# Two products for three in stick-breaking attention: the second parts of the split queries and values on the idle half of the array

## The chip, the cores and the metric

One core of one Trainium2 chip runs the whole program. The metric is the device time of one execution in microseconds (us); lower is better. Engines are named as in the profile: PE (TensorE matmul), PEld (its weight load), DVE (VectorE), ACT (ScalarE), POOL (GpSimd), SP (SyncE, which issues the loads).

## The reference

Two transformer blocks over 512 tokens of 1024 features. The first mixer runs stick-breaking attention (8 heads of 64) and HGRN2 (4 heads of 128) side by side and adds both, gated; the change touches the attention alone:

```
z = einsum('bhqd,bhkd->bhqk', qi, k) * scale        # blocks of 128 queries
log_beta = log_sigmoid(z)
log_rem = where(mask, log_beta - z, 0.0)            # mask: key before query
between = cumsum(log_rem, reverse) - log_rem
w = where(mask, exp(log_beta + between), 0.0)
o = einsum('bhqk,bhkd->bhqd', w, v)
```

After the first mixer come a squared-relu MLP, then the second block (MLA with a context, MLP, gMLP, MLP). None of that is edited.

## The kernel before

Activations lie feature-major, 128 features by 512 tokens. A float32 operand of a wide product is split into hi (12 significant bits) and lo = x - hi, and `mm3` (L180 to L185) adds hi.hi + hi.lo + lo.hi: three matmuls for one product. Weights come in granules of 128x1024; `wload` splits each with an ACT cast (`wh<-wr`) and a DVE subtraction (`wl<-wr,wh`).

The first mixer is `mixer_one` (L601). `feat` (L642) makes one feature tile: 24 matmuls into one of two PSUM banks (`ps`), then one DVE multiplication by the norm (`fiqg<-ps,rstd`, `qkv<-ps,rstd`, `gate<-ps,rstd`), which also frees the bank. `sb_pair` (L707) is one pair of attention heads (four pairs) in steps: `start` (L711) splits q, k and v; `weights` (L727) makes z of one head and one block of 128 queries with 128, 256, 384 or 512 keys (at least 256 columns are computed), its sigmoids, a DVE scan and a DVE product `b<-b,u`; `turn` (L746) transposes the weights on PE into `wT`; `product` (L756) splits `wT` tile by tile (512, 384, 256, 128 columns) and adds up `o`. A head has 64 features, half of the array's 128 rows. Before, q of a head lies in its half of two tiles, hi and lo, with zeros in the other half (`qz`), and v likewise (`vz`, half of the 128 columns zero), so that both heads add into the two halves of one bank `o`; one ACT copy (L769) takes it out.

`hgrn` (L814) is one head of HGRN2 in steps: features, gates (transposes `vt`), a DVE scan `bc` (L854), `edges` (transposes `kt`, products `sp`), scores `sc`. `branch` (L674) then splits the four `osb` tiles and multiplies them (`pg`).

The order of the steps is the string `ORDER` (L37), written by hand; from it a scheduler with a model of its own orders the queue of each engine. Each engine takes its queue strictly in order. Pools: `P()` is the ring of two `ps` banks, `O()` one of two banks for `z`, `vt`, `sp` and `sc`, and `o` has one bank.

Of the kernel before, what the change touches and what calls it, by code (L numbers as in the profile page):

```python
"""Two transformer blocks on one core.

The first block: stick-breaking attention and HGRN2 side by side, gated, then a squared-relu MLP and a
final norm.  The second: MLA with a context, then a gMLP mixer, each followed by a squared-relu MLP, all
modulated.  What the second block does to the context after its keys and values are taken never reaches
the output, so it is left out.

Activations lie feature-major, [128 features, 512 tokens].  A float32 operand x of a wide product is
split into hi = round(x) to 12 significant bits (the float32r format) and lo = x - hi, which is exact;
hi.hi + hi.lo + lo.hi is accumulated in float32.  Products with few columns run in plain float32.  # L10
"""
# [18 lines left out]
T = 512  # L30
TC = 256
EPS = 1e-6
#: The order in which the steps of the mixer take their turns: pairs of heads of the stick-breaking attention (S), heads
#: of HGRN2 (H), the gates of either branch (A, B) and their projections (G, M).
# [31 lines left out]
def cut(rs, c):  # L66
    """A part of the tokens of split operands."""
    return [(h[:, c], l[:, c]) for h, l in rs]
# [14 lines left out]
class Kernel:  # L83
# [5 lines left out]
    def S(self, n=T, dt=F32, name="t"):  # L89
        """A tile that may outlive the phase."""  # L90
        return self.sp.tile([128, n], dt, tag="s", name=name)

    def H(self, name="t"):
        """Half of the tokens, not for long."""
        return self.hp.tile([128, TC], F32, tag="h", name=name)

    def F(self, n=T, dt=F32, name="f", tag="f"):
        """A tile of the phase, 2 KB in each partition for the common tag."""
        return self.fp.tile([128, n], dt, tag=tag, name=name, bufs=self.tags.get(tag))
# [11 lines left out]
    def phase(self, name, banks, **tags):  # L111
        """Memory of a phase; banks, tags: how many tiles of each kind, in PSUM and in SBUF."""
# [29 lines left out]
    def split(self, x, gain=None, n=T, tag=None, eng=None):  # L142
        """x, times a gain by partition, in two parts."""
        if tag is None:
            hi, lo = self.S(n, F32R, "hi"), self.S(n, F32R, "lo")
        else:
            hi, lo = self.F(n, F32R, "hi", tag), self.F(n, F32R, "lo", tag)
        self.split_into(hi, lo, x, gain, eng)
        return hi, lo
# [7 lines left out]
    def wload(self, src):  # L157
        """One granule of weights, [128, up to 1024], split in two."""
# [7 lines left out]
    def wkeep(self, src):  # L166
        """The stationary operands of a granule that outlives the ring, in tiles of the phase."""
# [6 lines left out]
    def wsplit(self, w, k, c=128):  # L174
        """The stationary operands of k row tiles in a granule."""
# [3 lines left out]
    def mm3(self, out, ls, rs, start=True, stop=True):  # L179
        """out += sum over pairs of ls[i]^T rs[i], every operand a (hi, lo)."""  # L180
# [6 lines left out]
    # Where one layer's output becomes the next one's normed input, the products run half of the tokens at a time, in  # L187
    # a given order on the tensor engine, with the few products of the norm between them.
# [10 lines left out]
    def later(self, n, f):  # L199
        """Calls f after n more products of mm3."""  # L200
# [19 lines left out]
    class Sum:  # L220
        """A running sum of squares over the tiles of a feature-major array; with gains, [128, tiles, (1, gain^2)],
        also one of the squares times the gain's."""
# [18 lines left out]
        def half(self, x, z, m):  # L241
            """The same for half of the tokens of one of the last tiles."""
# [8 lines left out]
        def collect(self, out, z):  # L251
            """The sums over the features, in PSUM; two columns for each 128 tokens."""
# [10 lines left out]
    def sums(self, acc, n=T, bank=None):  # L263
        """The sums over the features of [128, n], tokens on partitions: two equal columns for each 128 tokens."""
# [5 lines left out]
    def rsqrt(self, out, x, d):  # L270
        """out = 1 / sqrt(x / d + eps) of a few columns."""
# [5 lines left out]
    def newton(self, out, a):  # L277
        """out = 1 / sqrt(a) of a few columns: a guess from the bits, then three steps of Newton's."""
# [8 lines left out]
    def spread(self, c, n=T, bank=None, i=0):  # L287
        """Columns, number i of two for each 128 tokens, along the free axis of every partition; in PSUM."""
# [8 lines left out]
    def rstd(self, acc, d, n=T, bank=None):  # L297
        """1 / sqrt(sum over features / d + eps), the same in every partition; in PSUM."""
# [4 lines left out]
    def mod_gain(self, norm, m, which):  # L303
        """norm * (1 + scale) as columns."""
# [7 lines left out]
    def first(self, ps, ws, xs):  # L312
        """Products of a few granules, half of the tokens at a time."""
# [6 lines left out]
    def down(self, srcs, rs, bank, residual, sums, done, whole=4, begun={}):  # L320
        """Output tiles, added to the residual; the last ones half of the tokens at a time.  sums: running sums of
        squares of the residual, with gains; done(z, columns) turns them into half of the next norm."""
# [38 lines left out]
    def renorm(self, norm, m, which):  # L361
        """What `down` calls when a half of the residual is complete: its modulated norm, in self.xs."""
# [11 lines left out]
    def modulate(self, out, xs, r, gains, shifts, c):  # L374
        """Part c of the tokens: (x * gain) * r + shift, split."""
# [12 lines left out]
    def context(self):  # L388
        """Latent keys and values of the context."""
# [49 lines left out]
    def ada(self, layer, lo, hi):  # L439
        """Columns lo..hi of the modulation of a layer, in granules of 128."""  # L440
# [19 lines left out]
    def mlp(self, w1, w2, xs, residual, scale=None, extra=None, down=None, halves=True):  # L460
        """residual(m, psum, tokens) is called with the four partial sums of every output tile."""
# [86 lines left out]
    def mlp_one(self):  # L548
# [30 lines left out]
        # y = h * gf * r goes on, r = 1 / sqrt(mean(h^2) + eps); for 1 / sqrt(mean(y^2) + eps) times r, which is  # L579
        # 1 / sqrt(mean((h * gf)^2) + eps (mean(h^2) + eps)), no second pass is needed  # L580
# [20 lines left out]
    def mixer_one(self):  # L601
        nc, tc, a = self.nc, self.tc, self.a
        xs, ssq, ws = [], self.Sum(self), {}
        # the first operands in pieces, two row tiles of three granules and of x at a time
# [13 lines left out]
        # the tensor engine's clock rises while the first operands are on their way  # L618
# [10 lines left out]
        # the first products, every tile of x as it comes  # L629
# [12 lines left out]
        def feat(m, name="u", tag="f"):  # L642
            """A feature tile of the input projection."""
# [9 lines left out]
        # stick-breaking attention  # L653
        qz = [self.F(T, F32R, "qz", "qv") for _ in range(4)]
        vz = [self.F(T, F32R, "vz", "qv") for _ in range(4)]
        for i in range(4):
            nc.gpsimd.memset((qz[i][64:128] if i < 2 else qz[i][0:64]).bitcast(F32), 0.0)
            o = 64 if i < 2 else 0
            nc.gpsimd.memset(vz[i].rearrange("p (t c) -> p t c", c=128)[:, :, o:o + 64].bitcast(F32), 0.0)
# [3 lines left out]
        for p in range(4):  # L663
            self.sb_pair(p, do, feat, qz, vz, osb)
            self.hgrn(p, do, feat, ohg)

        # the gates of either branch, what they let through of the first, and the sum
# [39 lines left out]
    def sb_pair(self, p, do, feat, qz, vz, out):  # L707
        """Two heads of the stick-breaking attention, in steps."""
        nc, s = self.nc, {}

        def start():  # L711
            q, k, v = s[0], s[1], s[2]
            s["ks"] = self.split(k, tag="sb")
            for h in range(2):
                c = slice(64 * h, 64 * h + 64)
                hi, lo = qz[2 * h], qz[2 * h + 1]
                self.act(hi[c], q[c], AF.Copy, scale=0.125)
                self.stt(lo[c], q[c], 0.125, hi[c].bitcast(F32), ALU.mult, ALU.subtract)
# [3 lines left out]
            for h in range(2):  # L722
                c = slice(64 * h, 64 * h + 64)
                hi, lo, src = (x.rearrange("p (t c) -> p t c", c=128)[:, :, c] for x in (*vz[2 * h:2 * h + 2], vt))
                self.split_into(hi, lo, src)

        def weights(h, i):  # L727
            ks = s["ks"]
# [4 lines left out]
            self.mm3(ps[:, :nn], [(qz[2 * h][:, c], qz[2 * h + 1][:, c])], [(ks[0][:, :nn], ks[1][:, :nn])])  # L733
# [12 lines left out]
        def turn(h, i):  # L746
            if i == 0:
                # transposed weights of the key tiles, 512, 384, 256 and 128 columns in three banks
# [7 lines left out]
        def product(h):  # L756
            if h == 0:
                s["o"] = self.Q("o", "o")
            o = s["o"]
            for j in range(4):  # L760
                n = T - 128 * j
                w = self.split(s["wT"][j][:, :n], n=n)
                vs = [(x.rearrange("p (t c) -> p t c", c=128)[:, j]) for x in vz[2 * h:2 * h + 2]]
                nc.tensor.matmul(o[:, 128 * j:], vs[0], w[0], start=h == 0 and j == 0, stop=False)
                nc.tensor.matmul(o[:, 128 * j:], vs[0], w[1], start=False, stop=False)
                nc.tensor.matmul(o[:, 128 * j:], vs[1], w[0], start=False, stop=h == 1 and j == 3)
            if h == 1:
                r = self.S(name="osb")
                nc.scalar.copy(r, o)  # L769
                self.tap("osb%d" % p, [o])  # L770
                out[p] = r
# [13 lines left out]
    def hgrn_begin(self):  # L785
# [12 lines left out]
        # the lower bound of the forget gate  # L798
# [15 lines left out]
    def hgrn(self, h, do, feat, out):  # L814
        """One head of HGRN2, in steps."""
# [26 lines left out]
        def decay():  # L842
            """Running sums of log f, in two parts for the range that the table takes."""
# [13 lines left out]
        def edges():  # L857
            q, k, b = s[2], s["k"], s["b"]
            # decays from and to the ends of a chunk
# [612 lines left out]
```

## Time and profile before

| what | value |
|---|---|
| runs | 2115.7, 2118.17, 2119.0 us; median 2118.17 |
| span of the profiled execution | 2115.3 us (first to last instruction; the 2.9 us to the median lie around it and between executions) |
| PE, DVE, ACT, POOL busy | 2074.1, 1342.9, 876.1, 216.3 us |
| chain that ended last | PE 87%, DVE 7%, ACT 3%, issue 2%, DMA 1% |
| mean granted clock of PE | 0.996 |

The profile records no device time of its own for the profiled execution, only the span. "Busy" is the time in which an engine has an instruction in flight. Matmuls are pipelined, so the cost of one in a dense run is the distance between the starts of two, not its duration. The windows give the busy time of each engine in a stretch; an engine's timeline gives its instructions one after the other, with the idle time before one and what ended it.

### The profile page before, as it was taken

The numbers are of one execution on the slowest core, as the hardware profiler recorded it, in microseconds if no ns is written. First come the engines' busy times: TensorE is split into PE (matmuls) and PEld (weight loads), VectorE is DVE, ScalarE is ACT, GpSimd is POOL, SyncE is SP. The second block draws the span as 40 slices with busy tenths as digits, with TensorE's granted clock in tenths as the row PEclk, the third lists the DMA queues.
The fourth block names the chain that finished last, engine by engine and source line by source line (L and its number), as shares of the span: only waits on it lengthen the run. The fifth ranks groups of instructions, "written<-read, shape, count | busy, mean of one in ns | idle before, by whom it ended". The sixth has DMA issues, their size and how long they took to land.

```text
span 2115.3 us, 27506 instructions
## 1 busy us (share of the span) xinstructions
PE 2074.1 (98%) x10550; PEld 1759.0 (83%) x10550; DVE 1342.9 (63%) x2482; ACT 876.1 (41%) x1430; POOL 216.3 (10%) x234
## 2 busy tenths in 40 slices
PE   9999999999999999899989999999999999999999
PEld 7888888878888888788878888888888889888887
DVE  6868775689675557888767766646456446434433
ACT  5546663354242324667645423223333324323221
POOL 0313220000000001345311000000000001000000
PEclk9999999999999999999999999999999999999999
DMA  5212122456556432101033655533222231222222
GB/s 173 70 60 66 49 84 63 155 177 208 168 189 199 159 110 87 38 18 36 31 130 112 202 194 196 192 130 119 81 99 80 90 120 61 100 99 91 100 100 80
DMA packets 73908, 238.69 MB, mean 113 GB/s; under 512 B 8240, under 2 KB 12592, under 8 KB 73776
## 3 DMA queue, kind: packets, MB, share of 16 engines
q1 hardware_dynamic: 73776, 236.93, 34.0%
q8 instruction: 83, 1.36, 0.3%
q14 instruction: 49, 0.40, 0.1%
HBM read 232.70 MB, written 4.19 MB: 112 GB/s over the span
## 4 chain that ended last, share of the span: by engine, by line
PE 87%; DVE 7%; ACT 3%; issue 2%; DMA 1%; POOL 0%; SPq 0%; ACTq 0%; DVEq 0%; POOLq 0%
PE pq L184 35%; PE ps L184 28%; PE po L184 13%; PE pg L184 2%; PE sc L215 1%; ACT pr L131 1%; PE pl L215 1%; DVE wl L125 1%; PE pq L215 1%; PE o L184 1%; DVE lo L125 1%; PE z L184 1%; DVE lo L128 1%; PE po L215 1%; PE pl L184 1%
## 5 line engine op out<-in xcount | busy, mean ns | idle before, releaser
L136 ACT CAST wh<-wr 128x1024 fp32r<-128x1024 f32 (+3 forms) x338 | 333.6, 990 | 850.0 <-PE pq L184 423.2
L125 DVE TENSOR_TENSOR wl<-wr,wh 128x1024 fp32r<-128x1024 f32 (+3 forms) x338 | 390.3, 1156 | 113.4 <-ACT wh L136 106.3
L184 PE MATMUL pq<-hi,wl 128*128 128x512 f32 (+1 forms) x880 | 336.2, 382 | 0.0
L184 PE MATMUL pq<-hi,wh 128*128 128x512 f32 (+1 forms) x880 | 336.1, 382 | 0.0
L184 PE MATMUL pq<-lo,wh 128*128 128x512 f32 (+1 forms) x880 | 336.0, 382 | 0.0
L184 PE MATMUL ps<-hl,wh 128*128 128x512 f32 (+1 forms) x752 | 227.6, 384 | 0.0
L184 PE MATMUL ps<-hi,wh 128*128 128x512 f32 x536 | 211.9, 396 | 4.1 <-ACT hi L131 2.1
L184 PE MATMUL ps<-hi,wl 128*128 128x512 f32 x536 | 211.5, 395 | 0.5 <-DVE wl L125 0.5
L184 PE MATMUL ps<-lo,wh 128*128 128x512 f32 x536 | 210.7, 393 | 0.0
L184 PEld LDWEIGHTS pq<-hi,wl 128*128 128x128 f32 x880 | 165.4, 188 | 32.3
L184 PEld LDWEIGHTS pq<-hi,wh 128*128 128x128 f32 x880 | 165.4, 188 | 32.2
L184 PEld LDWEIGHTS pq<-lo,wh 128*128 128x128 f32 x880 | 165.4, 188 | 32.2
L450 DVE SCALAR_TENSOR_TENSOR adaj<-ada,silu 128x1024 bf16<-128x1024 f32 x112 | 137.0, 1223 | 83.4 <-DMA ada<-in_ada 83.0
L128 DVE SCALAR_TENSOR_TENSOR x<-pq,m,x 128x512 f32<-128x512 f32 (+1 forms) x88 | 60.7, 690 | 198.2 <-PE pq L184 197.9
L184 PE MATMUL po<-hl,wh 128*128 128x512 f32 x528 | 163.8, 392 | 0.0
L184 PEld LDWEIGHTS ps<-hl,wh 128*128 128x128 f32 x752 | 139.0, 188 | 27.0
L125 POOL TENSOR_TENSOR hl<-mod,hl 128x256 fp32r<-128x256 f32 x36 | 30.1, 845 | 1164.7 <-ACT hl L382 945.9
L184 PE MATMUL ps<-hl,wl 128*128 128x512 f32 (+1 forms) x376 | 144.1, 383 | 0.0
L184 PEld LDWEIGHTS ps<-hi,wh 128*128 128x128 f32 x536 | 100.7, 188 | 26.2 <-ACT hi L131 2.5
L184 PEld LDWEIGHTS ps<-hi,wl 128*128 128x128 f32 x536 | 100.9, 188 | 22.3 <-DVE wl L125 1.0
L184 PEld LDWEIGHTS ps<-lo,wh 128*128 128x128 f32 x536 | 101.0, 188 | 20.2 <-DVE lo L125 0.4
L184 PEld LDWEIGHTS po<-hl,wh 128*128 128x128 f32 x528 | 99.5, 189 | 20.5
(375 smaller groups left out, 3832.1 us busy)
## 6 DMA issues: line engine op xcount, KB each, us to landing
wr<-in_f SPq DMA_DIRECT2D x128, 512.0 KB, 3.2
ada<-in_ada SPq DMA_DIRECT2D x96, 512.0 KB, 4.1
wr<-in_ff SPq DMA_DIRECT2D x64, 512.0 KB, 4.1
wr<-in_w_in SPq DMA_DIRECT2D x41, 512.0 KB, 3.5
wr<-in_gw_v SPq DMA_DIRECT2D x16, 512.0 KB, 3.2
wr<-in_gw_u SPq DMA_DIRECT2D x16, 512.0 KB, 3.2
wr<-in_gw_o SPq DMA_DIRECT2D x16, 512.0 KB, 3.2
wr<-in_w_out SPq DMA_DIRECT2D x8, 512.0 KB, 3.4
```

What stands on the lines that cost most here:

```text
L125: (eng or self.nc.vector).tensor_tensor(out=out, in0=a, in1=b, op=op)
L128: (eng or self.nc.vector).scalar_tensor_tensor(out=out, in0=a, scalar=s, in1=b, op0=op0, op1=op1)
L131: self.nc.scalar.activation(out=out, in_=x, func=func, scale=scale, bias=bias, **k)
L136: nc.scalar.copy(hi, x)
L184: self.nc.tensor.matmul(out, l, r, start=start and i == j == 0, stop=stop and i == n - 1 and j == 2)
L215: self.nc.tensor.matmul(out, l, r, start=start, stop=stop)
L450: nc.vector.scalar_tensor_tensor(out=d, in0=w, scalar=1.0, in1=s, op0=ALU.mult, op1=ALU.mult, accum_out=m[:, n:n + 1])
```

## The change

The idle half of a tile now carries the other part of the same operand. `qhl[h]` has q hi on the head's 64 partitions and q lo on the other 64. `kh[h]` has k hi on both halves, so one matmul gives q hi.k hi + q lo.k hi; a second one with `klz[h]` (k lo, zeros in the other half) adds q hi.k lo. `vhl[h]` has v hi in 64 columns and v lo in the other 64; one matmul with w hi and one with w lo give both parts in the two halves of PSUM, which are added while they are copied out (w lo.v lo comes along). Each head so takes a bank of its own, one after the other, since `o` still has one.

Counts: z takes 2 matmuls for 3 in 32 places, o likewise: 64 fewer on PE. Of these 32, the z ones have 256, 384 and 512 columns (16, 8, 8), the o ones 128, 256, 384 and 512 (8 each). DVE has 12 instructions more (per pair: `klz` twice where one `lo<-qkv,hi` stood, and two additions `osb<-o,ol`), ACT 18 more (per pair three more copies for `kh`, and two copies `ol<-o` for one `osb<-o`; two more table loads), POOL 6 memsets fewer. SP's loads are the same.

```
-        qz = [self.F(T, F32R, "qz", "qv") for _ in range(4)]
-        vz = [self.F(T, F32R, "vz", "qv") for _ in range(4)]
...
+        qhl, klz, vhl = ([self.F(T, F32R, n, "qv") for _ in range(2)] for n in ("qhl", "klz", "vhl"))
+        for h in range(2):
+            nc.gpsimd.memset(klz[h][64 - 64 * h:128 - 64 * h].bitcast(F32), 0.0)
...
         def start():
-            s["ks"] = self.split(k, tag="sb")
+            s["kh"] = [self.F(T, F32R, "kh", "sb") for _ in range(2)]
             for h in range(2):
-                c = slice(64 * h, 64 * h + 64)
-                hi, lo = qz[2 * h], qz[2 * h + 1]
-                self.act(hi[c], q[c], AF.Copy, scale=0.125)
-                self.stt(lo[c], q[c], 0.125, hi[c].bitcast(F32), ALU.mult, ALU.subtract)
+                c, e = slice(64 * h, 64 * h + 64), slice(64 - 64 * h, 128 - 64 * h)
+                kh, x = s["kh"][h], qhl[h]
+                nc.scalar.copy(kh[c], k[c])
+                nc.scalar.copy(kh[e], k[c])
+                self.tt(klz[h][c], k[c], kh[c].bitcast(F32), ALU.subtract)
+                self.act(x[c], q[c], AF.Copy, scale=0.125)
+                self.stt(x[e], q[c], 0.125, x[c].bitcast(F32), ALU.mult, ALU.subtract)
...
-            self.mm3(ps[:, :nn], [(qz[2 * h][:, c], qz[2 * h + 1][:, c])], [(ks[0][:, :nn], ks[1][:, :nn])])
+            self.mm(ps[:, :nn], qhl[h][:, c], s["kh"][h][:, :nn], True, False)
+            self.mm(ps[:, :nn], qhl[h][:, c], klz[h][:, :nn], False, True)
...
         def product(h):
             if h == 0:
-                s["o"] = self.Q("o", "o")
-            o = s["o"]
+                out[p] = self.S(name="osb")
+            o = self.Q("o", "o")
             for j in range(4):
                 n = T - 128 * j
                 w = self.split(s["wT"][j][:, :n], n=n)
-                vs = [(x.rearrange("p (t c) -> p t c", c=128)[:, j]) for x in vz[2 * h:2 * h + 2]]
-                nc.tensor.matmul(o[:, 128 * j:], vs[0], w[0], start=h == 0 and j == 0, stop=False)
-                nc.tensor.matmul(o[:, 128 * j:], vs[0], w[1], start=False, stop=False)
-                nc.tensor.matmul(o[:, 128 * j:], vs[1], w[0], start=False, stop=h == 1 and j == 3)
-            if h == 1:
-                r = self.S(name="osb")
-                nc.scalar.copy(r, o)
-                self.tap("osb%d" % p, [o])
-                out[p] = r
+                for i in range(2):
+                    self.mm(o[:, 128 * j:], vhl[h][:, 128 * j:128 * j + 128], w[i], i == j == 0, i == 1 and j == 3)
+            t = self.S(name="ol")[0:64]
+            nc.scalar.copy(t, o[64:128])
+            self.tt(out[p][64 * h:64 * h + 64], o[0:64], t, ALU.add)
```

The edit shifts what the scheduler makes of `ORDER`, and instructions that are not edited stand elsewhere. The PE queue differs through the whole first mixer, a little in the first MLP, and in the first heads of MLA (there the 256-column products of the values come ahead of the first scores `pl`, where 384-column products of the queries stood); from there to the end it is the same.

First place, PE in the third pair of heads: the product of its second head and the small HGRN2 products after it (`vt` of `qkv` is the next pair's). Before, the product follows a long run of feature products `ps`, whose last row stands first here:

```order
L184 MATMUL ps<-hi,wl 128x512
L764 MATMUL o<-hi,vz 128x512
L765 MATMUL o<-lo,vz 128x512
L766 MATMUL o<-hi,vz 128x512
L764 MATMUL o<-hi,vz 128x384
L721 MATMUL vt<-ident,qkv 128x128 x4
L875 MATMUL kt<-ident,d 128x128 x3
L765 MATMUL o<-lo,vz 128x384
L766 MATMUL o<-hi,vz 128x384
L764 MATMUL o<-hi,vz 128x256
L765 MATMUL o<-lo,vz 128x256
L766 MATMUL o<-hi,vz 128x256
```

In the change the product of the first head (its last row stands first here), the transposes and the product of the second, `kt`, `sp` and `sc` follow each other:

```order
L215 MATMUL o<-lo,vhl 128x128
L824 MATMUL vt<-ident,fiqg 128x128 x4
L755 MATMUL wT<-ident,b 128x128 x7
L215 MATMUL o<-hi,vhl 128x512
...
L215 MATMUL o<-hi,vhl 128x128
L215 MATMUL o<-lo,vhl 128x128
L873 MATMUL kt<-ident,d 128x128 x3
L215 MATMUL sp<-fiqg,kd 128x128 x3
L215 MATMUL sc<-fiqg,k 128x128 x4
L184 MATMUL ps<-hi,wh 128x512
L184 MATMUL ps<-lo,wh 128x512
```

Behind that stand the same feature products as before, 24 and more. The `ps` rows that stood between the two heads' products have moved ahead of the first head's product.

Second place, DVE in the same stretch, up to the multiplication that frees a `ps` bank (last row; the scan over `reset` prints as SCALAR_TENSOR_TENSOR). Before:

```order
L854 SCALAR_TENSOR_TENSOR bc<-reset,fiqg 128x512
L125 TENSOR_TENSOR qe<-fiqg,eb 128x512
L125 TENSOR_TENSOR d<-bc 128x512
L125 TENSOR_TENSOR wl<-wr,wh 128x1024
L125 TENSOR_TENSOR lo<-wT,hi 128x512
L125 TENSOR_TENSOR d<-d,k 128x512
L125 TENSOR_TENSOR lo<-wT,hi 128x384
L125 TENSOR_TENSOR lo<-wT,hi 128x256
L125 TENSOR_TENSOR lo<-wT,hi 128x128
L125 TENSOR_TENSOR wl<-wr,wh 128x1024
L125 TENSOR_TENSOR vz<-vt,vz 128x4x64
L125 TENSOR_TENSOR fiqg<-ps,rstd 128x512
```

In the change:

```order
L125 TENSOR_TENSOR lo<-wT,hi 128x384
L125 TENSOR_TENSOR fiqg<-fiqg,f_1763 128x512
L125 TENSOR_TENSOR lo<-wT,hi 128x256
L125 TENSOR_TENSOR lo<-wT,hi 128x128
L852 SCALAR_TENSOR_TENSOR bc<-reset,fiqg 128x512
L125 TENSOR_TENSOR vhl<-vt,vhl 128x4x64
L125 TENSOR_TENSOR qe<-fiqg,eb 128x512
L125 TENSOR_TENSOR d<-bc 128x512
L125 TENSOR_TENSOR osb<-o,ol 64x512
L125 TENSOR_TENSOR vhl<-vt,vhl 128x4x64
L125 TENSOR_TENSOR d<-d,k 128x512
L125 TENSOR_TENSOR fiqg<-ps,rstd 128x512
```

The weight subtractions `wl<-wr,wh` have moved away, most of them ahead; two additions `osb<-o,ol` (one of them a few rows above this piece) and one more `vhl<-vt,vhl` stand ahead of the bank's release. The two `lo<-wT,hi` of 512 and 384 columns now stand ahead of the scan `bc`.

Third place, PE at the end of the last pair, from the last products of `o` to the first `pg` that takes the pair's own `osb`. Before:

```order
L765 MATMUL o<-lo,vz 128x128
L766 MATMUL o<-hi,vz 128x128
L184 MATMUL pg<-hi,wh 128x512
L184 MATMUL pg<-lo,wh 128x512
L184 MATMUL pg<-hi,wl 128x512
...
L184 MATMUL pg<-hi,wl 128x512
L875 MATMUL kt<-ident,d 128x128 x3
L184 MATMUL pg<-hi,wh 128x512 x2
L184 MATMUL pg<-lo,wh 128x512
```

In the change:

```order
L184 MATMUL pg<-hi,wl 128x512
L215 MATMUL o<-lo,vhl 128x128
L873 MATMUL kt<-ident,d 128x128 x3
L215 MATMUL sp<-fiqg,kd 128x128 x3
L215 MATMUL sc<-fiqg,k 128x128 x4
L184 MATMUL pg<-hi,wh 128x512 x2
L184 MATMUL pg<-lo,wh 128x512
L184 MATMUL pg<-hi,wl 128x512
```

Before, twelve `pg` products of the other `osb` tiles stand between the last `o` and `kt` (eight of them in the rows left out); in the change they stand ahead of the last `o`, and only `kt`, `sp` and `sc` follow it.

## Rows read from the trace of the kernel before

**Rows 1.** The page: the span, and the engines' busy time.

```profile
span 2115.3 us, 27506 instructions
...
PE 2074.1 (98%) x10550; PEld 1759.0 (83%) x10550; DVE 1342.9 (63%) x2482; ACT 876.1 (41%) x1430; POOL 216.3 (10%) x234
```

**Rows 2.** Windows: us, then PE, PEld, DVE, ACT, POOL busy, PEclk, DMA share, GB/s.

```profile
40.00:350.00 310.00, 308.99 (x1652) 263.56 (x1651) 232.49 (x408) 176.53 (x289) 79.99 (x124) 1.00 0.21 66
168.00:191.00 23.00, 22.69 (x124) 19.23 (x123) 20.55 (x32) 15.97 (x29) 8.70 (x12) 1.00 0.19 63
```

**Rows 3.** Timeline of PE, first head's product: start, duration, engine, line, operation.

```profile
65.89 0.40 PE L766 MATMUL o<-hi,vz 128*128 128x512 f32 x1
66.12 0.34 PE L764 MATMUL o<-hi,vz 128*128 128x384 f32 x1
...
66.66 0.28 PE L764 MATMUL o<-hi,vz 128*128 128x256 f32 x1
...
67.02 0.22 PE L764 MATMUL o<-hi,vz 128*128 128x128 f32 x1
...
67.30 0.29 PE L753 MATMUL wT<-ident,b 128*128 128x128 f32 x1
```

**Rows 4.** Tiles z and o: one of the three matmuls, its count and sizes.

```profile
L184 PE MATMUL z<-lo,qz x32: 276/332/480, 46.3 to 239.8; 128*128 128x256 f32 x16, 128*128 128x384 f32 x8, 128*128 128x512 f32 x8
```

```profile
L766 PE MATMUL o<-hi,vz x32: 272/310/397, 65.9 to 256.3; 128*128 128x512 f32 x8, 128*128 128x384 f32 x8, 128*128 128x256 f32 x8, 128*128 128x128 f32 x8
```

**Rows 5.** Groups on DVE and ACT, 40 to 345 us: count, busy us, mean ns.

```profile
L125 DVE TENSOR_TENSOR wl<-wr,wh 128x1024 fp32r<-128x1024 f32 x35 | 44.4, 1270 | 6.9 <-ACT wh L136 6.9
...
L125 DVE TENSOR_TENSOR fiqg<-ps,rstd 128x512 f32<-128x512 f32 x15 | 10.1, 681 | 5.3 <-PE ps L184 5.2
...
L128 DVE SCALAR_TENSOR_TENSOR qz<-qkv,qz 64x512 fp32r<-64x512 f32 x8 | 5.9, 742 | 0.1
...
L125 DVE TENSOR_TENSOR vz<-vt,vz 128x256 fp32r<-128x256 f32 x8 | 3.3, 410 | 1.4 <-ACT vz L136 1.4
```

```profile
L131 ACT ACT_TABLE_LOAD x28 | 35.9, 1283 | 1.0 <-DVE f L848 0.5
```

**Rows 6.** Timeline of PE, third pair: first head's last transposes; first `ps` of a new bank.

```profile
165.28 0.60 PE L753 MATMUL wT<-ident,b 128*128 128x128 f32 x4
165.63 0.48 PE L184 MATMUL ps<-hi,wh 128*128 128x512 f32 x1
...
191.06 0.48 PE L184 MATMUL ps<-hi,wh 128*128 128x512 f32 x1
```

**Rows 7.** Timeline of DVE over the same stretch; in brackets idle time and its releaser.

```profile
168.02 1.76 DVE L125 TENSOR_TENSOR lo<-wT,hi 128x512 fp32r<-128x512 f32 x4
...
188.80 1.22 DVE L125 TENSOR_TENSOR wl<-wr,wh 128x1024 fp32r<-128x1024 f32 x1 [0.65 <-ACT wh L136]
...
190.27 0.68 DVE L125 TENSOR_TENSOR fiqg<-ps,rstd 128x512 f32<-128x512 f32 x1
```

**Rows 8.** Timeline of ACT and DVE at the end of the last pair.

```profile
257.30 0.57 ACT L769 COPY osb<-o 128x512 f32<-128x512 f32 x1
...
257.90 0.62 ACT L136 CAST hi<-osb 128x512 fp32r<-128x512 f32 x1
...
258.80 0.68 DVE L125 TENSOR_TENSOR lo<-osb,hi 128x512 fp32r<-128x512 f32 x1
```

**Rows 9.** Windows around two idle stretches of PE; the column after POOL is PEclk.

```profile
432.00:436.00 4.00, 1.90 (x10) 1.06 (x9) 3.14 (x5) 3.53 (x6) 0.00 (x0) 1.00 0.83 316
436.00:442.00 6.00, 6.00 (x23) 4.86 (x23) 5.97 (x17) 5.12 (x13) 0.00 (x0) 0.72 0.65 228
1118.00:1128.00 10.00, 6.00 (x32) 6.01 (x33) 6.22 (x20) 1.79 (x4) 0.00 (x0) 0.66 0.16 53
```

**Rows 10.** Windows in MLA: its first heads, and the 80 us after them.

```profile
860.00:940.00 80.00, 70.12 (x478) 61.96 (x477) 66.85 (x185) 51.33 (x115) 32.69 (x19) 1.00 0.09 27
940.00:1020.00 80.00, 77.10 (x530) 69.64 (x529) 68.64 (x188) 57.07 (x138) 45.30 (x27) 1.00 0.13 40
```

More of the change, by code (lines that the diff above doesn't have):

```diff
@@ L651, in feat @@
             return t
-        qz = [self.F(T, F32R, "qz", "qv") for _ in range(4)]
-        vz = [self.F(T, F32R, "vz", "qv") for _ in range(4)]
[L656 to L659, printed above, removed]
+        qhl, klz, vhl = ([self.F(T, F32R, n, "qv") for _ in range(2)] for n in ("qhl", "klz", "vhl"))
+        for h in range(2):
+            nc.gpsimd.memset(klz[h][64 - 64 * h:128 - 64 * h].bitcast(F32), 0.0)
         osb, ohg, merged = [None] * 4, [None] * 4, []
@@ L663, in mixer_one @@
         for p in range(4):
-            self.sb_pair(p, do, feat, qz, vz, osb)
+            self.sb_pair(p, do, feat, qhl, klz, vhl, osb)
             self.hgrn(p, do, feat, ohg)
@@ L705, in mixer_one, with sb_pair @@
             self.x.append(x)
-    def sb_pair(self, p, do, feat, qz, vz, out):
+    def sb_pair(self, p, do, feat, qhl, klz, vhl, out):
         nc, s = self.nc, {}
@@ L722, in start @@
             for h in range(2):
-                c = slice(64 * h, 64 * h + 64)
-                hi, lo, src = (x.rearrange("p (t c) -> p t c", c=128)[:, :, c] for x in (*vz[2 * h:2 * h + 2], vt))
-                self.split_into(hi, lo, src)
+                x = vhl[h].rearrange("p (t c) -> p t c", c=128)
+                self.split_into(x[:, :, 0:64], x[:, :, 64:128],
+                                vt.rearrange("p (t c) -> p t c", c=128)[:, :, 64 * h:64 * h + 64])
         def weights(h, i):
-            ks = s["ks"]
             n = 128 * (i + 1)
```

## The prediction

> **What bounds the kernel now.** The page comes first: PE is busy 2074.1 of 2115.3 us [rows 1], so a matmul removed from a dense stretch is worth its whole pitch, unless something else then arrives late. What else is near its limit is read from windows over the edited stretch. In the first mixer, 40 to 350 us, PE is busy 308.99 of 310 us and DVE 232.49: on average DVE has 77 us to spare. But from 168 to 191 us DVE is busy 20.55 of 23.0 us [rows 2], and there it decides, by the timelines: DVE ends the multiplication that frees a `ps` bank at 190.27 + 0.68 = 190.95 [rows 7], and the `ps` product that needs the bank starts at 191.06 [rows 6], 0.1 us later. PE was dense there only because the scheduler had put enough `ps` products ahead. The question is whether that still holds when PE gets there sooner.
>
> **What is removed.** The pitch of a matmul is the distance of starts in the dense product of one head: 0.23 us for 512 columns, three of 384 in 0.54 (0.18 each), three of 256 in 0.36 (0.12), three of 128 in 0.28 (0.09) [rows 3]. One of three goes at each place [rows 4]: for z 8 x 0.23 + 8 x 0.18 + 16 x 0.12 = 5.2 us, for o 8 x (0.23 + 0.18 + 0.12 + 0.09) = 5.0 us; together **-10.2 us**, 2.55 in each pair of heads. The new matmuls have the shapes of the old ones, so they keep these pitches.
> The Trainium skill, TensorE: Matmul & The Clock Gate, section on the back-to-back issue gap, gives a sustained 131 ns for a matmul of 512 columns and 81 ns for one of 128; on a straight line between them the 64 would be worth an estimated 6.9 us. The rows show 0.23 and 0.09, so the measurement decides; by the page's figures the removal would be 3.3 us smaller.
>
> **What is added off PE.** DVE has 12 instructions more, of 64 partitions and 512 columns. No row shows such an addition out of PSUM; the nearest are the `fiqg` multiplication at 0.68 and the `qz` one at 0.74 us, above, and the `vz` one of 256 columns at 0.41, below [rows 5]. I take 0.68 less the overlap of neighbours, 0.6: 7 us in all, bounds 5 to 9. ACT has 16 more copies of about the same size, 10 us, and two table loads of 1.28 [rows 5]. Spread over the mixer both fit under PE [rows 2] and cost nothing; what they cost is paid where DVE's queue is waited for. The six memsets on POOL go from the start, where nobody waits for them: 0.
>
> **The third pair, where it is paid.** By the order, the feature products that stood between the two heads' products now stand ahead of the first. From the last transposes of the first head (call their start T; 165.28 before, [rows 6]) PE now has only this until the first `ps` of a new bank: 10 `ps` products (2.3 us), 4 of z (0.8), 16 of o (2.5), 25 transposes at 0.09 (four take 0.35 [rows 6]; 2.2) and 7 small plain products of HGRN2, twice a transpose at the least (1.3): 9.1 us, where it had 25.8. If PE is dense up to T, all it does up to that `ps` is the work of before less three pairs' removal (7.6 us), so T = 191.06 - 7.6 - 9.1 = 174.4 us.
> DVE cannot be that quick. After T come the transposes (0.35) and an ACT cast (0.6), so `lo<-wT` starts at T + 1.0 at the earliest; before it was T + 2.7 [rows 6, 7]. From there to the end of the bank's release DVE took 190.95 - 168.02 = 22.9 us, of which 20.55 busy. In the change this piece of the queue has two `wl<-wr,wh` fewer (2 x 1.2, the third one's wait of 0.65 for the cast [rows 7] may go as well), one `qkv<-ps` fewer (0.6), two additions more (1.2) and one `vhl` more (0.3): -1.5. So 19.1 us if it never waits, 21.4 with the waits of before. I take 19.7, near the dense end, since the operands of the first half are there early, but the two ACT steps around `bc` still have their table loads. The `ps` then starts at 174.4 + 1.0 + 19.7 + 0.1 = 195.2 us: 4.1 later than before, after a stall of 195.2 - 183.5 = 11.7 us. The ends: 194.6 and, with T + 2.7 and all waits, 198.6.
> A second count bounds it without T: up to that release DVE's queue has the instructions of before and 10 of 0.6 us (4 `klz`, where 4 `lo<-qkv` went and the 8 of q stay; 6 additions), one early `lo<-osb` and one `vhl` more, 6.9 us: if DVE had no slack ahead, 191.06 + 6.9 = 198.0; if its slack took all, 191.06.
> So of the 7.6 us removed up to there nothing is left, and 4.1 us more are lost: **+11.7 us**, bounds 7.6 to 15.1.
> The Trainium skill, TensorEngine Tiling (Array Packing), section on the PSUM bottleneck, warns that packing the array speeds up TensorE but not the evacuation of PSUM, which may become the bound. The average over the mixer speaks against it (232.49 of 310), the stretch of 23 us for it: by the average the sum would be 2109, by the stretch it is the one here.
>
> **The last pair.** Its 2.55 us are in the 10.2. But the chain behind the last `o` is longer. Before: copy, cast, subtraction, 0.57 + 0.62 + 0.68 = 1.9 us [rows 8], under 12 `pg` products (2.7 us). Now an addition of 0.68 comes in, 2.6 us, and by the order only 3 transposes and the 7 small products (1.6 us) cover it. **+1.2 us**, bounds 0 (if the last `o` comes late itself) and 2.6.
>
> **The clock.** Where PE idled 2.1 of 4 us at 432 us, the 6 us after show a granted clock of 0.72: 1.7 us lost; at 1118 us, 4 idle of 10 us at 0.66: 3.4 us lost [rows 9]. Full speed is 2.4 GHz, and in such stretches part runs at 1.2. A stall of 11.7 us in the third pair is longer than both, but lies before DVE's release, so part of the loss falls into the wait. I take **+1.2**, bounds 0 and 5.1 (both prices).
>
> **Sum.** -10.2 + 11.7 + 1.2 + 1.2 = +3.9 us. The sum stands against the profiled execution (2115.3 us); the median of the runs is 2118.17, 2.9 above its span, and I add it there: **2122.1 us**. A measurement of this kernel can tell about 0.2%, 4.2 us, from no change: faster means under 2113.9, slower over 2122.4. The forecast lies inside, at the upper edge. Its own range is 2118 to 2126.
>
> **Rivals.**
> *PE stays dense.* DVE's 77 us of slack before and after the third pair let it run ahead, or the stretch is shorter than the chain I drew. For it: the average. Against it: the release stands 29 instructions behind the first head's `lo<-wT`, and this cannot begin before PE's own transposes. Then only the last pair's wait is paid: 2118.2 - 10.2 + 1.2 = 2109.
> *The clock falls in the stall and stays down behind it.* Place: the first `ps` products after the wait in the third pair; price 5.1 us in place of 1.2, and the matmuls that DVE waits for inside the stall (transposes and products, some 6 us at full speed) run at half, up to 3 us more. It decides if the idle time falls in one piece behind the small products rather than in short ones between them. 2122.1 + 3.9 and up to 3 more: 2126 to 2129, slower.
> *The order of the first MLA heads decides.* Its PE queue is changed though nothing there is edited. PE idles 80 - 70.12 = 9.9 us from 860 to 940 us and 2.9 in the next 80 [rows 10]: 7 us that an order could win, or lose again. Either sign: 2115 to 2129.
> That the matmuls do not go is excluded by the order: 64 fewer rows of `z` and `o`.
>
> **Chances.** The forecast 0.50 (0.36 within 0.2%, 0.14 above it, since the edge is so near); PE dense 0.17 (0.16 faster); clock 0.22 (0.21 slower); MLA's order 0.11 (0.01 faster, 0.04 same, 0.06 slower). The rest of the second and third, 0.01 each, is no change. Together: faster 0.17, same 0.42, slower 0.41. The range runs from PE dense, 2109, to the clock's middle price, 2128; about 0.08 is left out below, where a better order of MLA adds to it, and 0.10 above.
>
> **What would show it.** Right: in the third pair one idle stretch of PE, or several within 20 us, of 9 to 15 us in all, ended by the DVE release `fiqg<-ps,rstd`; the first `ps` behind it at 194 to 199 us; DVE busy over 0.9 of that stretch; 64 fewer matmuls at pitches of 0.09 to 0.23; about 1 us idle ahead of `pg` in the last pair; a granted clock under 1 around 195 us. Wrong: PE busy 99% from 40 to 340 us and everything behind the mixer some 9 us earlier; or the difference made after 400 us.

## The result and the profile after

| | median us | runs | span of the profiled execution |
|---|---|---|---|
| before | 2118.59 | 4, 2115.7 to 2119.29 | 2115.3 |
| the change | 2141.43 | 4, 2140.47 to 2144.06 | 2142.3 |

The ratio is 1.0112 (95% interval 1.0100 to 1.0124): 22.8 us slower, 1.1%. The forecast was 2122.1 us in a range of 2109 to 2128. With the 10.2 us of removed matmuls, some 33 us were lost, of which the sum held 14.1 (11.7, 1.2 and 1.2). The profiled execution of the change is the slowest of the four, 2.6 us above their median, and the two spans differ by 27.0 us, 4 more than the medians.

The page of the changed kernel, beside [rows 1]:

```profile
span 2142.3 us, 27398 instructions
...
PE 2081.1 (97%) x10486; PEld 1763.5 (82%) x10486; DVE 1352.9 (63%) x2494; ACT 890.5 (42%) x1448; POOL 211.0 (10%) x228
```

There are 64 matmuls fewer, and yet PE is busy 7.0 us longer; DVE is busy 10.0 us longer, ACT 14.4. The windows say where (columns as in [rows 2]):

```profile
40.00:350.00 310.00, 287.67 (x1444) 240.18 (x1444) 229.74 (x383) 180.81 (x293) 78.31 (x124) 0.95 0.20 61
80.00:120.00 40.00, 35.69 (x183) 29.79 (x182) 27.36 (x53) 13.58 (x23) 11.15 (x15) 0.87 0.17 48
...
180.00:220.00 40.00, 29.20 (x135) 23.69 (x134) 29.47 (x51) 23.06 (x43) 13.17 (x20) 0.79 0.09 27
260.00:300.00 40.00, 35.04 (x167) 28.41 (x166) 31.94 (x61) 26.30 (x39) 8.17 (x13) 0.96 0.18 53
```

The last three stretches before:

```profile
80.00:120.00 40.00, 39.35 (x220) 33.45 (x219) 28.11 (x56) 14.42 (x23) 5.74 (x7) 1.00 0.25 79
...
180.00:220.00 40.00, 39.69 (x215) 34.00 (x214) 29.72 (x52) 24.78 (x40) 13.11 (x20) 1.00 0.19 60
...
260.00:300.00 40.00, 40.00 (x217) 34.34 (x216) 31.14 (x55) 29.68 (x40) 10.63 (x13) 1.00 0.25 79
```

In the first mixer PE now idles 22.3 of 310 us, where it idled 1.0 [rows 2], and its granted clock is 0.95 where it was 1.00. Most of the idle time (20.1 of 22.3 us) lies in the three stretches shown, near 85, near 200 and near 280 us, and in each of them the clock is lower than before (0.87, 0.79 and 0.96 for 1.00). The end of the mixer, the last `pg` products, before and after:

```profile
L184 PE MATMUL pg<-hi,wl x64: 388/392/478, 254.5 to 388.0; 128*128 128x512 f32 x64
```

```profile
L184 PE MATMUL pg<-hi,wl x64: 388/390/476, 275.7 to 413.5; 128*128 128x512 f32 x64
```

The last one starts 25.5 us later; the whole execution is 27.0 us longer. So all but 1.5 us of the loss lies in the mixer, where 35.7 us went (25.5 and the 10.2 removed): 21.3 more idle, and the remaining 14.4 is about what the lower clock accounts for (0.05 of it over 310 us is 15.5 us). An estimate by place, idle time above that of before plus the missing clock times the length of the window: near 85 us 3.7 + 5.2 = 8.9, from 120 to 180 us 2.3, near 200 us 10.5 + 8.4 = 18.9, near 280 us 5.0 + 1.6 = 6.6; together 36.7.

Third pair of heads, timeline of PE in the changed kernel, from the first head's last transposes (165.28 before, [rows 6]) to the next `ps` of a new bank (191.06 before):

```profile
183.88 0.60 PE L755 MATMUL wT<-ident,b 128*128 128x128 f32 x4
...
190.72 0.66 PE L824 MATMUL vt<-ident,fiqg 128*128 128x128 f32 x4 [1.62 <-ACT b L131]
192.66 0.55 PE L755 MATMUL wT<-ident,b 128*128 128x128 f32 x3 [1.28 <-DVE b L125]
194.80 1.11 PE L755 MATMUL wT<-ident,b 128*128 128x128 f32 x4 [1.60 <-DVE b L125]
...
200.45 0.41 PE L215 MATMUL o<-lo,vhl 128*128 128x128 f32 x1
205.84 0.91 PE L873 MATMUL kt<-ident,d 128*128 128x128 f32 x3 [4.98 <-DVE d L125]
207.31 1.65 PE L215 MATMUL sp<-fiqg,kd 128*128 128x128 f32 x6 [0.57 <-ACT kd L875]
208.75 1.92 PE L215 MATMUL sc<-fiqg,k 128*128 128x128 f32 x8
210.32 0.78 PE L184 MATMUL ps<-hi,wh 128*128 128x512 f32 x1
```

and DVE over the same stretch, beside [rows 7]:

```profile
184.93 1.77 DVE L125 TENSOR_TENSOR lo<-wT,hi 128x512 fp32r<-128x512 f32 x4
...
205.10 0.68 DVE L125 TENSOR_TENSOR d<-d,k 128x512 f32<-128x512 f32 x1
205.70 0.69 DVE L125 TENSOR_TENSOR fiqg<-ps,rstd 128x512 f32<-128x512 f32 x1
```

From 189.1 us, the end of a run of `o` products, to the `ps` PE has nothing but a chain of small steps, most of which wait for DVE or ACT. The longest wait, 4.98 us, is for `d`, which `kt` transposes; the bank's release ends at 206.39, but the `ps` that needs it stands behind `kt`, `sp` and `sc` in PE's queue and starts 3.9 us later. From 194.8 us on PE is at the lower of its two clocks, 1.2 GHz, after it had idled 4.5 of the 5.7 us before; a 512-column matmul or a transpose takes up to twice as long, and the granted clock is 0.50 through to the `ps`:

```profile
194.80:210.32 15.52, 9.22 (x34) 7.15 (x34) 10.72 (x20) 9.49 (x18) 5.79 (x8) 0.50 0.00 0
```

What PE waited for in the mixer, the first four rows (engine, line, waited for: us, times, longest):

```profile
PE kt L873 <- DVE d L125: 8.3, 3, 5.0
PE wT L755 <- DVE b L125: 2.9, 2, 1.6
PE ps L184 <- DVE fiqg L125: 2.7, 3, 1.5
PE o L215 <- DVE lo L125: 2.0, 2, 1.5
```

`kt`, the first PE step of a chunk behind DVE's chain in HGRN2, heads the list, and it does so in three heads, not in one. The single bank of `o`, which now passes from one head to the other, is not among the waits.

### The profile page after: what moved, and what is told of

It reads as the page before. It is cut to its first block, busy times and chain, and to the rows that moved or that the text cites. A ratio compares the mean times of both kernels' runs of the same rounds, so it can differ in the third digit from the quotient of the medians.

```text
span 2142.3 us, 27398 instructions
## 1 busy us (share of the span) xinstructions
PE 2081.1 (97%) x10486; PEld 1763.5 (82%) x10486; DVE 1352.9 (63%) x2494; ACT 890.5 (42%) x1448; POOL 211.0 (10%) x228
## 4 chain that ended last, share of the span: by engine, by line
PE 86%; DVE 7%; ACT 3%; issue 2%; DMA 1%; POOL 0%; SPq 0%; ACTq 0%; DVEq 0%; POOLq 0%
PE pq L184 34%; PE ps L184 29%; PE po L184 13%; PE pg L184 2%; PE sc L215 1%; PE pl L215 1%; ACT pr L131 1%; DVE wl L125 1%; DVE lo L125 1%; PE pq L215 1%; PE pl L184 1%; PE po L215 1%; PE o L184 1%; PE ps L215 1%; PE o L215 1%
```

## The experiments

Two theories. **Order:** the scheduler remakes the queues whenever the work changes; the written order of steps suits the old queues, and in the new ones PE comes to places where only dependent steps are left in its queue. **Work:** the added DVE and ACT instructions are what PE waits for.

**The two parts apart.** The first keeps the product as it was, the second z:

```
 z_alone:  z = qhl.kh + qhl.klz;   o += vz_hi.w_hi + vz_hi.w_lo + vz_lo.w_hi   (as before)
 o_alone:  z = mm3(qz, ks)  (as before);   o = vhl.w_hi + vhl.w_lo, copy and add
```

> The z part of the change alone: z with 2 matmuls for 3, the product of weights and values as before (3 matmuls, one bank for both heads, one ACT copy). 32 matmuls fewer than before (5.2 us), DVE 4 and ACT 12 copies more. Order theory (the loss of the change is PE waiting at a few places where its remade queue has no feature products left between two dependent steps): the queue is remade here too, so most of the loss is here already, 5 to 20 us slower than before, with PE idle again near 90 and near 200 us. Work theory (the added DVE and ACT work is what PE waits for): a third of the DVE work and two thirds of the ACT work are here, so the losses of this part and of the other add up to the 22.8 us of the change; this one between 0 and 10 us.

> The product part of the change alone: weights by values with 2 matmuls for 3, a bank for each head, copy and addition on the way out; z as before. 32 matmuls fewer (5.0 us), DVE 8 additions more, ACT 4 copies more. Order theory: again most of the loss by itself, 10 to 30 us slower than before, so that the two parts together would give clearly more than 22.8 us, over 30. Work theory: the two parts add up to 22.8 us, within 4.

| kernel | median us (lowest to highest) | ratio to before (95%) |
|---|---|---|
| z_alone | 2128.45 (2126.7 to 2128.99) | 1.0052 (1.0030 to 1.0075) |
| o_alone | 2140.02 (2137.81 to 2142.24) | 1.0108 (1.0079 to 1.0138) |

Against 2117.04 us for before: 11.4 and 23.0 us slower, 34.4 together, where both at once cost 22.8. The parts don't add up, though the intervals are wide (6.4 to 15.9 and 16.7 to 29.2 us): the product part alone costs as much as the whole, though it removes half of the matmuls and adds 8 of the 12 DVE instructions and few of ACT's. Windows from 180 to 220 us, z_alone first:

```profile
180.00:220.00 40.00, 33.66 (x179) 28.50 (x179) 28.60 (x51) 25.02 (x40) 14.93 (x22) 0.91 0.14 47
```

```profile
180.00:220.00 40.00, 29.93 (x135) 24.19 (x134) 27.79 (x50) 21.69 (x40) 11.47 (x19) 0.74 0.09 27
```

Both lose in the same place, but not by the same waits: `o` of z_alone waits 3.9 us for `hi` and 1.5 for `lo` of its weights there, o_alone has the wait of `kt` for `d` (5.0 us).

**The same work in another order.** In the kernel before, two neighbours of `ORDER` are exchanged:

```
-S2t7 H1f3 H1a H1c S2v1 H1b H1d H1e H1l7 S3f2 S3a H1l3 H2f3 S3z0 H1l2 S3t0 S3z1 H1l4 H1l6 S3z2 H3f0 H1l0 S3t1
+S2t7 H1f3 H1a S2v1 H1c H1b H1d H1e H1l7 S3f2 S3a H1l3 H2f3 S3z0 H1l2 S3t0 S3z1 H1l4 H1l6 S3z2 H3f0 H1l0 S3t1
```

> The kernel before with two neighbouring steps exchanged in its written order: in the third pair, the product of the second head ahead of one HGRN2 step that stood ahead of it. Not one instruction more or fewer. Order theory: 5 to 20 us slower than before, with PE idle around 180 to 215 us and a granted clock under 1 there. Work theory: the same work, so within 3 us of before.

Measured: 2135.45 us (2132.48 to 2138.42), ratio 1.0087 (1.0053 to 1.0120): 18.4 us slower, without one step more; the scheduler's new queues differ from the old ones in more than the two steps, and ACT loads a table 34 times instead of 32 (1.28 us each; from 172 to 212 us, around the stall, 4 loads where before had 6). Its windows and first wait:

```profile
80.00:120.00 40.00, 39.35 (x225) 33.61 (x224) 27.84 (x55) 13.77 (x23) 4.75 (x6) 1.00 0.23 77
180.00:220.00 40.00, 29.14 (x147) 24.61 (x146) 22.72 (x40) 20.55 (x31) 11.18 (x17) 0.83 0.11 34
```

```profile
PE kt L875 <- DVE d L125: 9.9, 1, 9.9
```

This is the picture of the change in its third pair (29.14 us busy against 29.20, a clock of 0.83 against 0.79, a wait of `kt` for `d`, 9.9 us in one piece here and 5.0 there), and nowhere else: 80 to 120 us is as before. So such a stall needs no added work.

**The DVE additions taken away.**

```
-            t = self.S(name="ol")[0:64]
-            nc.scalar.copy(t, o[64:128])
-            self.tt(out[p][64 * h:64 * h + 64], o[0:64], t, ALU.add)
+            nc.scalar.copy(out[p][64 * h:64 * h + 64], o[0:64])
```

> The change without its eight DVE additions: the second half of each product (weights by the lo part of the values) is left out of the result, and one ACT copy of 64 partitions takes the first half out. DVE has 8 instructions of 0.6 us fewer than the change, and each pair's result is ready one step earlier. Work theory: over half of the 22.8 us comes back. Order theory: under 5 us comes back, and PE still waits near 90 and near 200 us.

Measured: 2143.19 us (2142.91 to 2143.47), ratio 1.0123. Nothing comes back: `kt` still waits 8.8 us for `d`, in three waits. This speaks against the work theory, but does not settle it by itself, since the queues are remade here too (`wT` now waits 4.9 us for `b` where it waited 2.9), and what the 5.5 us of additions gave back could have been lost to that. What settles it has to keep the work and change the order.

**The order fitted to the new queues.** Other written orders for the steps of the change. In the third pair, for example, refit2 has the HGRN2 chain ahead of the second head's product:

```
-S2t6 H1f2 S2t7 H1f3 H1a H1c S2v1 H1b H1d H1e H1l7 S3f2 S3a
+S2z7 H1a S3f0 H1c H1b S2t6 H1d H1e H1l7 H1l6 S2t7 S2v1 H1l4 H1l2 S3a
```

and the rest of the mixer is moved too. refit is an earlier one of the kind, with this in the same place:

```
+H1a S3f1 H1c S2v0 S3f2 H3f3 S2t4 H1b S2t5 S2z6 S2t6 S2z7 H1d S2t7 S2v1 H1e H1l7 H1l3 S3a
```

refit_pool has an order of its own and moves half of each weight subtraction of the feature products to POOL; before_pool has this move alone, in the old code and order:

```
-        self.split_into(hi, lo, raw)
+            self.nc.scalar.copy(hi, raw)
+            for i in range(2):
+                c = slice(512 * i, 512 * i + 512)
+                self.tt(lo[:, c], raw[:, c], hi[:, c].bitcast(F32), ALU.subtract, eng if i else None)
```

(refit_pool, like refit, took the output tiles of the projection in another sequence and so computed with permuted tiles; the amount of work is the same.)

> The change with its steps in another written order, fitted to the new queues; every step's code is that of the change, no instruction more or fewer. Order theory: most of the 33 us that PE waits or runs at half speed more than before comes back: 15 to 25 us faster than the change, so 2115 to 2126, with PE idle under 4 us at each place. Work theory: DVE and ACT have the same work, so PE waits about as long: over 2132.

> The change, again in another written order, and half of each weight subtraction of the feature products (512 of 1024 columns, 38 granules) on POOL, which is idle three quarters of the mixer; DVE has some 20 us less to do there. Order theory together with DVE as what PE waits for where no feature product is left: PE almost dense, so nearly the whole 10.2 us of the removed matmuls shows: 2108 to 2114, faster than before. Work theory (ACT's copies count as much): ACT is as loaded as in the change, so no faster than 2125.

> The control for the last: the kernel before with the same half of each weight subtraction on POOL, order as before. PE is dense there (308.99 of 310 us), so both theories expect nothing to win: within 4 us of before, or slower if the relieved DVE queue is remade for the worse.

> The change with its steps in another written order, fitted to its own queues; the code of every step is that of the change. In the order of refit the eight output tiles of the projection were taken in another sequence, so that it computed with permuted tiles; here they stand in sequence. Order theory: all but a few us of what PE lost comes back: 2113 to 2121, no more than 3 us of idle at any of the three places. Work theory: 2130 or more.

> The kernel before with the written order of refit2: three products each, none of the added DVE and ACT work. Order theory: an order fits one set of queues, so here the old kernel is the one that loses, 5 to 20 us slower than before, and slower than refit2. Work theory (an order that serves the larger work serves the smaller too): within 4 us of before or faster.

| kernel | median us (lowest to highest) | before, beside it | ratio (95%) |
|---|---|---|---|
| refit | 2125.87 (2125.78 to 2129.41) | 2118.37 | 1.0036 (1.0021 to 1.0050) |
| refit_pool | 2125.12 (2123.62 to 2126.10) | 2118.37 | 1.0031 (1.0019 to 1.0043) |
| before_pool | 2125.41 (2124.35 to 2126.59) | 2118.37 | 1.0033 (1.0018 to 1.0048) |
| refit2 | 2122.73 (2120.43 to 2124.89) | 2116.95 | 1.0028 (1.0017 to 1.0040) |
| before_refit2 | 2136.42 (2135.74 to 2137.09) | 2116.95 | 1.0093 (1.0074 to 1.0111) |

With all of its added work, the change loses 18.7 us of its time by order alone (2141.43 to 2122.73; 17.0 when each is set against the old kernel beside it, 22.8 less 5.8). As an account of the 22.8 us the work theory falls here. And the cross: with the old code, the order of refit2 is 19.5 us slower than the old order, with the new code 18.7 us faster.

| | old order | order of refit2 |
|---|---|---|
| old code | 2116.95 (2118.59 beside the change) | 2136.42 |
| code of the change | 2141.43 | 2122.73 |

So, each against the old code beside it, the change is worth +22.8 us under one order and -13.7 under the other; neither number belongs to the matmuls alone. The windows of refit2, to be read against those of the change above:

```profile
40.00:350.00 310.00, 302.66 (x1573) 256.66 (x1574) 243.54 (x407) 186.30 (x302) 77.17 (x124) 0.99 0.21 66
80.00:120.00 40.00, 36.79 (x202) 31.99 (x201) 32.19 (x60) 17.14 (x31) 15.01 (x22) 0.91 0.13 41
180.00:220.00 40.00, 36.86 (x204) 31.43 (x203) 33.74 (x56) 23.78 (x41) 13.62 (x19) 1.00 0.19 60
260.00:300.00 40.00, 40.00 (x214) 34.23 (x213) 32.35 (x51) 30.82 (x40) 12.07 (x14) 1.00 0.22 66
```

The idle time of 310 us falls from 22.3 to 7.3, the clock is back at 0.99. What is left sits in HGRN2's scores:

```profile
PE sc L216 <- DVE x L126: 5.9, 4, 2.6
```

The expected "no more than 3 us of idle at any of the three places" held at the last alone (0.0 at 260 to 300 us); 3.2 and 3.1 are left at the others, and refit2 is 5.8 us slower than before, 1.7 above its expected 2121. refit came out at the upper end of its 2115 to 2126, with 5.7 and 5.8 us of idle at the first two places where under 4 were expected; of refit_pool the expected 2108 to 2114 did not come, for a reason that stands at the end. No order tried made the change faster than the kernel before, so that one exists is not shown. Between refit2 and the 10.2 us of the removed matmuls lie 16.0 us; how much of them a better order would bring back, and how much is the price of the added work, stays open. before_pool is 7.0 us slower than before, with PE idle 7.0 us in the mixer.

## Why the prediction was wrong, by its steps

- *What bounds the kernel:* right for its place. The stretch that DVE decides is the one where the change lost most, and the exchange of two steps reproduces it. **The step that failed** is the sum over the mixer. The order of PE was followed in the third and the last pair only, and the sum holds one large stall where there were three; the other places stand at nothing without a reason, and cost an estimated 8.9 us near 85 us and 2.3 from 120 to 180 us. And the clock, at 1.2 us, was the term most mis-sized: some 15 us. The stall that the sum lacks is near 85 us: `kt` of the first HGRN2 head there waits for `d`, and the next `ps` for its bank.

```profile
84.07 0.55 PE L873 MATMUL kt<-ident,d 128*128 128x128 f32 x3 [1.27 <-DVE d L125]
85.18 1.31 PE L215 MATMUL sp<-fiqg,kd 128*128 128x128 f32 x6 [0.57 <-ACT kd L875]
...
89.67 0.79 PE L184 MATMUL ps<-hi,wh 128*128 128x512 f32 x1 [1.47 <-DVE fiqg L125]
```

- *What is removed,* 10.2 us: not contradicted; under the order of refit2 the new code is 13.7 us faster than the old, though that holds what the order costs the old code too.
- *What is added off PE:* the single sizes held. The additions took 0.683 us (0.68 taken, 0.6 net of overlap), the copies `ol<-o` on ACT 0.582; DVE's total rose by 10.0 us, above the bounds of 5 to 9. That all this "costs nothing" by itself is not shown. The additions:

```profile
L125 DVE TENSOR_TENSOR osb<-o,ol 64x512 f32<-64x512 f32 x8 | 5.5, 683 | 4.2 <-ACT ol L768 4.0
```

- *The third pair, where it is paid:* by the estimate above it cost 18.9 us, where the sum had 11.7 and 1.2 for the clock. The idle time itself came out near, in part by luck: from T to the `ps` PE idled 10.8 us (11.7 forecast), but in seven waits, none of which the bank's release ended; and its 9.1 us of work took 15.7, most of it at the lower clock. `lo<-wT` began 1.05 us after the transposes (1.0 forecast), and the DVE piece from there to the release took 206.39 - 184.93 = 21.5 us (19.7 taken, 21.4 as the upper end). But the sum let the `ps` start 0.1 us after the release; by the order that stands in the document itself, `kt`, `sp` and `sc` come first, and `kt` needs `d`, which DVE makes one instruction ahead of the release. With the clock at half the `ps` started 3.9 us behind it. From T to the `ps` it is 26.4 us instead of 20.8. And T was 183.88, not 174.4: the place near 85 us and the 2.3 us of idle from 120 to 180 us, 11.2 together by the estimate, had put everything back before.
- *The last pair:* 1.2 us forecast; from 260 to 300 us PE idles 5.0 us and the clock is 0.96, an estimated 6.6 us. The forecast priced the copy, addition, cast and subtraction behind the last `o` (279.91), and for these PE did not wait: `pg` follows `sc` without a gap at 286.14. It waited ahead of the last `o` for the parts of `wT`, and behind it once more for `d`; of neither the sum had a term:

```profile
274.11 0.49 PE L215 MATMUL o<-lo,vhl 128*128 128x512 f32 x1 [1.48 <-DVE lo L125]
...
282.20 0.55 PE L873 MATMUL kt<-ident,d 128*128 128x128 f32 x3 [2.07 <-DVE d L125]
```

- *The clock:* 1.2 us taken, 5.1 as the upper end; 0.05 of 310 us is 15.5. The rows used [rows 9] were of single idle stretches; here PE stayed at the lower clock from 194.8 us to the `ps`, through waits of 0.2 to 5.0 us with small matmuls between them, and steps that ACT waited for in turn took longer (four transposes 1.11 us instead of 0.60).
- *The rivals:* the clock rival had the mechanism right (steps inside the stall at half speed), with 3.9 to 6.9 us more for it in one place; its condition, idle time in one piece behind the small products, did not come. MLA's order did not decide: the whole difference behind the mixer is 1.5 us. PE did not stay dense.
- The rule of the Trainium skill, TensorEngine Tiling (Array Packing), section on the PSUM bottleneck, which was weighed as the side of the short stretch, fits the 3.9 us that `ps` waited for its banks (2.7 of it behind `fiqg`, 0.9 behind `qkv`, 0.3 behind `gate`); the largest waits, `kt` for `d` and `wT` for `b`, are no evacuation.

## What to carry to other kernels

Where a scheduler orders the queues from a written order of steps, a removed matmul is not worth its pitch and an added copy not its duration: first read the new queue of the bound engine from end to end for runs of steps that depend on each other with nothing independent between, and follow every one of them, not the first that is found. An edit and an order are one design: measure the edit under an order fitted to it as well (here +22.8 us became +5.8), and take an exchange of two neighbours in the old order as the yardstick (18.4 us) for what the order alone can do. Where the clock falls in a stall, count more than its idle time: here 35.7 us were lost for 21.3 idle.

## What was not expected of the hardware

Moving half of the weight subtractions to POOL won nothing, not even on DVE, which is busy 1348.9 us in before_pool and 1342.9 before. A DVE instruction whose two operands both lie in SBUF became longer, and one that reads PSUM did not. DVE in refit_pool:

```profile
L126 DVE TENSOR_TENSOR wl<-wr,wh 128x512 fp32r<-128x512 f32 x42 | 40.8, 971 | 2.8 <-ACT wh L167 2.7
L126 DVE TENSOR_TENSOR x<-x,k 128x256 f32<-128x256 f32 x28 | 16.6, 591 | 5.7 <-ACT x L132 5.7
L126 DVE TENSOR_TENSOR fiqg<-ps,rstd 128x512 f32<-128x512 f32 x14 | 9.6, 684 | 2.9 <-PE ps L191 2.9
```

and POOL there:

```profile
L126 POOL TENSOR_TENSOR wl<-wr,wh 128x512 fp32r<-128x512 f32 x34 | 51.9, 1526 | 97.0 <-ACT wh L167 83.6 <-DVE fiqg L126 5.4 <-DVE d L126 3.5
```

The whole subtraction of 1024 columns took 1.270 us on DVE [rows 5]; its half now takes 0.971 there and 1.526 on POOL. The one multiplication out of PSUM kept its 0.68 [rows 5]. refit_pool has another order than before; before_pool has the same. The subtraction of 512 columns on DVE, in before and then in before_pool:

```profile
L125 DVE TENSOR_TENSOR wl<-wr,wh 128x512 fp32r<-128x512 f32 x9 | 6.5, 720 | 0.0
```

```profile
L125 DVE TENSOR_TENSOR wl<-wr,wh 128x512 fp32r<-128x512 f32 x41 | 40.0, 976 | 6.2 <-ACT wh L166 6.1
```

The multiplication `x<-x,k` of 256 columns takes 0.429 us in before, 0.544 in before_pool and 0.591 in refit_pool. The trace of before_pool also shows when: the subtraction takes 0.68 us on average where no POOL instruction runs at the same time (9 of the 41) and 1.06 where one does (32); `x<-x,k` 0.42 (14) and 0.67 (14). The Trainium skill, GPSIMD Engine Reference, section Specifications, says that the two engines share their way to SBUF and that DVE instructions with two SBUF inputs contend there; the rows agree, and show the size.
